# A matmul with rotary embedding: a first read of 64 bytes from every 16th weight row, and weight chunks loaded and multiplied in turn with the first four tiles

## The chip, the cores and the metric

The kernel runs on one core of a Trainium2 chip. The metric is the device time in microseconds of one execution; the median of 13 runs of the kernel before is 154.45 us, from 153.99 to 156.54.

## The reference

```
y = x @ weight                      # x: 16 x 512 x 768, weight: 768 x 768, float32
y -> (batch, seq, 12 heads, 64);  y1, y2 = halves of the 64
out1 = y1 * cos[:, :32] - y2 * sin[:, :32]
out2 = y2 * cos[:, 32:] + y1 * sin[:, 32:]
out  = concat(out1, out2)           # 16 x 512 x 768, float32
```

cos and sin are 512 x 64 and depend on the place in the sequence alone.

## The kernel before, in words

The 8192 rows of x are cut into 64 tiles of 128 rows, handled as 32 pairs. Tile (n, s) is half s of pair n: batch 2 * (n // 4) + s, rows n % 4, n % 4 + 4, and so on. The two tiles of a pair need the same rows of cos and sin.

A tile takes these steps. It is loaded in float32 (`load`, L83, issued on SyncE), cast to float16 (`cast`, L76 on ScalarE, ACT, or L78 on VectorE, DVE), transposed in six blocks on TensorE, PE (`transpose`, L140) and copied from PSUM back to SBUF (L76 or L78). Then six matmuls of 768 columns each, one for each chunk of 128 weight rows, add up in PSUM (`mm`, L177; each is split where a PSUM bank ends, so a tile and a chunk make two instructions). DVE multiplies the result by cos and sin (`products`, L187), GpSimd (POOL) adds the two products (`add`, L204), and a DMA stores the pair (L249). Some later pairs are loaded in another layout and transposed by DVE (L148).

The weight is needed whole: six chunks, named by (t, e), each made of every sixth weight row, (p, t, e) -> row 6p + 2t + e. A chunk is loaded in float32 (`load_w`, L123, SyncE) and cast to float16 on DVE (`cast_w`, L126). So the first tiles can't be finished before the sixth chunk has landed.

Every instruction stands in the order in which the program writes it, on each engine's own queue. DMAs issued on SyncE use eight semaphores in rotation, so from some point on an issue waits until an earlier load has landed. The order of the head is written out by hand:

- SyncE issues x(0,0), x(0,1), x(1,0), x(1,1), then chunk 0 in two parts (columns 0 to 255, then the rest), chunks 1 to 5, cos, sin, and then x(2,0), x(2,1) and so on.
- PE starts with `warm` matmuls on zeros (L259), which compute nothing that is used. They go on between the first transposes, 17 in all.
- Tiles (0,0) and (1,0) are cast and copied by DVE, (0,1) and (1,1) by ACT.
- As each chunk is cast, PE multiplies tiles (0,0) and (0,1) with it, and from the second chunk on also (1,0) with an earlier chunk. What remains of (1,0) and all of (1,1) follows after the sixth chunk. Before the last three chunks of (1,1), `upto("turn", 5)` transposes tile (2,0).

PSUM has six banks for results, three for a pair; pair 2 takes those of pair 0 once DVE has read them. From pair 2 on a loop goes through the pairs; the change does not touch it. POOL reads one column of tile (3,0) (`mark`, L336) before it issues its own first loads (L99) and begins with the additions.

Of the kernel before, what the change touches and what calls it, by code (L numbers as in the profile page):

```python
# [10 lines left out]
FP32 = mybir.dt.float32  # L11
# [6 lines left out]
def kernel(  # L18
# [9 lines left out]
    nc = tc.nc  # L28
    P = nc.NUM_PARTITIONS

    B, S, H = x.shape
# [9 lines left out]
    CHUNKS = [(t, e) for t in range(NT) for e in range(2)]  # L41
# [9 lines left out]
    def where(n, s):  # L51
        return 2 * (n // SB) + s, n % SB

    konst = ctx.enter_context(tc.tile_pool(name="konst", bufs=1))
    ident = konst.tile([P, P], FP16)
    mark = konst.tile([P, 1], FP32)
    cold = konst.tile([P, 512], FP16)
    sin_sb = konst.tile([P, SB, D], FP32)
    csn = konst.tile([P, 2, SB, D], FP32)
# [12 lines left out]
    w_raw, xss, xhs, x16, xTT, psys, tqs, ovs = {}, {}, {}, {}, {}, {}, {}, {}  # L72

    def copy(eng, o, i_):
        if eng is nc.scalar:
            eng.copy(out=o, in_=i_)  # L76
        else:
            eng.tensor_copy(out=o, in_=i_)  # L78

    def load(n, s):  # L80
        b, r = where(n, s)
        xss[n, s] = xpool.tile([P, H], FP32, tag="xs", name="xs")
        nc.sync.dma_start(  # L83
            out=xss[n, s], in_=x[b].rearrange("(p r) h -> r p h", r=SB)[r]
        )

    def load_pair(n):
        for s in (0, 1):
            if n < NP and n not in BLOCKS and n not in BLOCKS_SP:
                load(n, s)  # L90
# [29 lines left out]
    def load_w(t, e, c0=0, c1=H):  # L120
        if c0 == 0:
            w_raw[t, e] = bpool.tile([P, H], FP32, tag="xh", name="w_raw")
        nc.sync.dma_start(out=w_raw[t, e][:, c0:c1], in_=wv[t, e, :, c0:c1])  # L123

    def cast_w(t, e, c0=0, c1=H):
        nc.vector.tensor_copy(out=w_sb[:, t, e, c0:c1], in_=w_raw[t, e][:, c0:c1])  # L126

    def cast(n, s, eng):
        xc = cpool.tile([P, H], FP16, tag="xc", name="xc")
        x16[n, s] = xc  # L130
        src = xss.pop((n, s))
        src = src.rearrange("p (m t e) -> p t m e", t=NT, e=2)
        copy(eng, xc.rearrange("p (t m e) -> p t m e", t=NT, e=2), src)

    def transpose(n, s, eng):
        xc = x16.pop((n, s)).rearrange("p (t m e) -> p t e m", t=NT, e=2)
        bank = pt_pool.tile([P, 8, P], FP16, tag="pt", name="pt")
        pt = bank[:, 0 : 2 * NT].rearrange("p (t e) m -> p t e m", e=2)
        for t, e in CHUNKS:
            nc.tensor.transpose(pt[:, t, e, :], xc[:, t, e, :], ident)  # L140
        xT = tpool.tile([P, NT, 2, P], FP16, tag="xT", name="xT")
        copy(eng, xT, pt)
        xTT[n, s] = xT
# [13 lines left out]
    def psum(n, s):  # L157
        key, banks = (n, 3) if n < NP - ALONE else ((n, s), 2)
        if (n, s) == (NP - 1, 1):
            key, banks = (n, s), 3  # L160
        if key not in psys:
            psys[key] = [
                py_pool.tile([P, 512], FP32, tag="psy", name="psy") for _ in range(banks)
            ]
        ps = psys[key]
        if n >= NP - ALONE:
            cuts = (0, HH, H) if banks == 2 else (0, 5 * D, 10 * D, H)
            return [(b[:, 0 : hi - lo], lo, hi) for b, lo, hi in zip(ps, cuts, cuts[1:])]
        cut = 512 if s == 0 else 256
        return [(ps[s][:, ds(s * 256, cut)], 0, cut), (ps[s + 1][:, 0 : H - cut], cut, H)]  # L170

    def mm(n, s, t, e, c0=0, c1=H):
        for k, (ps, lo, hi) in enumerate(psum(n, s)):
            a, z = max(c0, lo), min(c1, hi)
            if a >= z:
                continue
            nc.tensor.matmul(  # L177
                ps[:, a - lo : z - lo],
                xTT[n, s][:, t, e, :],
                w_sb[:, t, e, a:z],  # L180
                start=((t, e) == CHUNKS[0] and n > 1),
                stop=((t, e) == CHUNKS[-1] and (n > 1 or s >= k)),
            )
# [65 lines left out]
        eng.dma_start(out=dst, in_=src)  # L249


    WARM = 17
    opened = [0]

    def warm(k):
        for _ in range(k):
            n, b = divmod(opened[0] % 6, 3)
            psum(n, 0)
            nc.tensor.matmul(  # L259
                psys[n][b], cold[:, 0:P], cold, start=True, stop=opened[0] < WARM - 6  # L260
            )
            opened[0] += 1

    ctx.enter_context(tc.manual_schedule())

    nc.vector.memset(cold, 0.0)  # L266
    nc.gpsimd.memset(ident, 0.0)  # L267
    nc.gpsimd.affine_select(
        out=ident,
        in_=ident,  # L270
# [3 lines left out]
        pattern=[[-1, P]],  # L274
        channel_multiplier=1,
    )
    for n in (0, 1):
        load_pair(n)
    load_w(0, 0, 0, 256)
    load_w(0, 0, 256, H)  # L280
    for t, e in CHUNKS[1:]:
        load_w(t, e)
    nc.sync.dma_start(out=csn[:, 0], in_=cos.rearrange("(p r) d -> p r d", r=SB))
    nc.sync.dma_start(out=sin_sb, in_=sin.rearrange("(p r) d -> p r d", r=SB))
    for n in range(2, AHEAD - 1):
# [7 lines left out]
    def upto(what, k):  # L293
        while done[what] < min(k, 2 * NP):
            n, s = divmod(done[what], 2)
            done[what] += 1
            if what == "cast":
                if n not in BLOCKS:
                    cast(n, s, nc.scalar)
            elif n in BLOCKS or n in BLOCKS_SP:  # L300
                transpose_blocks(n, s)
            else:
                transpose(n, s, nc.scalar)
# [4 lines left out]
    transpose(0, 0, nc.vector)  # L308
    warm(2)
    transpose(0, 1, nc.scalar)  # L310
    cast(1, 0, nc.vector)
    cast(1, 1, nc.scalar)
    warm(2)
    transpose(1, 0, nc.vector)
    warm(3)
    for c0, c1 in ((0, 256), (256, H)):
        cast_w(0, 0, c0, c1)
        mm(0, 0, 0, 0, c0, c1)
        mm(0, 1, 0, 0, c0, c1)
        if c0 == 0:  # L320
            transpose(1, 1, nc.scalar)
    for k, c in enumerate(CHUNKS[1:]):
        cast_w(*c)
        if k < 2:
            mm(1, 0, *CHUNKS[k])
        mm(0, 0, *c)
        mm(0, 1, *c)
        if 1 < k < 4:
            mm(1, 0, *CHUNKS[k])

    nc.vector.tensor_copy(out=csn[:, 1, :, 0:HD], in_=sin_sb[:, :, HD:D])  # L331
    nc.vector.tensor_scalar_mul(
        out=csn[:, 1, :, HD:D], in0=sin_sb[:, :, 0:HD], scalar1=-1.0
# [4 lines left out]
    load_blocks(BLOCKS[0], (1, 3))  # L338
    rope_pair(0)
    upto("cast", 6)  # L340
    for c in CHUNKS[4:]:
        mm(1, 0, *c)
    for c in CHUNKS[:3]:
        mm(1, 1, *c)
    upto("turn", 5)
    for c in CHUNKS[3:]:
        mm(1, 1, *c)
# [2 lines left out]
    for n in range(2, NP):  # L350
# [7 lines left out]
        for s in (0, 1):  # L358
# [18 lines left out]
            for ps, lo, hi in psum(n, s):  # L377
                for c in CHUNKS:
                    mm(n, s, *c, lo, hi)
                c0, c1 = s * H + lo, s * H + hi  # L380
# [55 lines left out]
```

## Time and profile before

| | |
|---|---|
| median of 13 runs | 154.45 us |
| profiled execution, its time | 154.64 us |
| its span in the profile | 152.9 us |
| PE busy | 145.3 us, 95% |
| DVE busy | 131.1 us, 86% |
| POOL busy | 123.8 us, 81% |
| ACT busy | 73.6 us, 48% |
| DMA | 51.17 MB, mean 335 GB/s |

The span runs from the first instruction to the last; the execution's own time is 1.7 us longer. In the profile a row names the line, the engine, the operation and the tiles it writes and reads; "SPq" is an issue on SyncE's queue, "PEld" the loading of a stationary operand, and the words in square brackets tell how long the engine was idle before and what ended that. The table of windows gives, for each stretch, the busy time of PE, PEld, DVE, ACT and POOL with the number of instructions, then the granted clock of TensorE, the busy share of the DMA engines and the GB/s they moved.

### The profile page before, as it was taken

To read this page: it belongs to the slowest core of one execution; us is meant where nothing else is said; L and a number is where in the kernel's file an instruction comes from. 1 tells how busy PE (TensorE), PEld (TensorE's weight loads), DVE (VectorE), ACT (ScalarE), POOL (GpSimd) and SP (SyncE) were. 2 spreads that over 40 slices of the span, in tenths; PEclk is the share of its full clock that TensorE was granted. 3 is DMA by queue.
4 is the path that set the end of the run, shared out by engine and by line. 5 is a ranking of instruction groups with operands and counts; after the bars stand their busy time and mean duration, and the time that the engine had idled before them with its cause. 6 is when DMAs were issued, how large, how long until landed. Compare 5 with 4: busy or idle time off the path is not lost.

```text
span 152.9 us, 2731 instructions
## 1 busy us (share of the span) xinstructions
PE 145.3 (95%) x1044; PEld 92.4 (60%) x1044; DVE 131.1 (86%) x141; ACT 73.6 (48%) x91; POOL 123.8 (81%) x69
## 2 busy tenths in 40 slices
PE   6989999999999999999999999999999999999950
PEld 2455678665666566666666566666656666666640
DVE  0556999779898998989898989989898989997890
ACT  3340686884344826183535726282616648765200
POOL 1000199999998999799997999787897879999990
PEclk9999999999999999999999999999999999999999
DMA  4999999999999999999999999999999999997554
GB/s 145 350 403 397 404 321 248 296 350 365 331 248 410 322 338 344 337 397 298 370 326 358 379 351 318 358 382 406 264 301 409 414 410 412 412 363 277 219 203 151
DMA packets 29037, 51.17 MB, mean 335 GB/s; under 512 B 7264, under 2 KB 14944, under 8 KB 29024
## 3 DMA queue, kind: packets, MB, share of 16 engines
q1 hardware_dynamic: 16640, 29.04, 56.8%
q10 hardware_dynamic: 6944, 19.99, 33.1%
q0 software_dynamic: 5440, 1.97, 10.7%
q8 instruction: 8, 0.13, 0.3%
q14 instruction: 5, 0.04, 0.1%
HBM read 27.79 MB, written 25.17 MB: 346 GB/s over the span
## 4 chain that ended last, share of the span: by engine, by line
PE 80%; POOL 7%; DMA 5%; SPq 3%; DVE 2%; POOLq 1%; issue 0%; DVEq 0%
PE psy L177 73%; PE pt L140 7%; POOL ov L204 7%; DMA w_raw<-in_weight_dram 5%; SPq L123 1%; DVE tq L187 1%; SPq L83 1%; POOLq L431 1%; DVE w_sb L126 0%; POOLq L204 0%; DVEq L187 0%
## 5 line engine op out<-in xcount | busy, mean ns | idle before, releaser
L177 PE MATMUL psy<-w_sb,xT 128*128 128x256 f16 (+3 forms) x787 | 131.5, 322 | 0.6 <-DVE w_sb L126 0.6
L187 DVE TENSOR_TENSOR tq<-psy,csn 128x1024 f32<-128x1024 f32 (+2 forms) x100 | 112.2, 1164 | 9.4 <-PE psy L177 9.1
L204 POOL TENSOR_TENSOR ov<-tq 128x1536 f32<-128x1536 f32 (+3 forms) x42 | 111.6, 2679 | 7.8 <-DVE tq L187 5.2
L177 PEld LDWEIGHTS <-xT 128*128 128x128 f16 x787 | 75.2, 98 | 45.3 <-issue 0.8
L76 ACT COPY xT<-pt 128x768 f16<-128x768 f16 x38 | 30.4, 799 | 58.6 <-PE pt L140 58.6
L76 ACT CAST xc<-xs 128x768 f16<-128x768 f32 x38 | 33.0, 903 | 9.5 <-DMA xs<-in_x_dram 8.8
L140 PE MATMUL pt<-ident,xc 128*128 128x128 f16 x240 | 20.2, 221 | 0.5 <-DVE xc L78 0.5
L140 PEld LDWEIGHTS <-xc 128*128 128x128 f16 x240 | 16.9, 99 | 6.2 <-DVE xc L78 1.5
L336 POOL COPY mark<-xs 128x1 f32<-128x1 f32 x1 | 0.2, 185 | 16.6 <-DMA xs<-in_x_dram 16.6
L76 ACT CAST xc<-xf 128x768 f16<-128x768 f32 x14 | 12.7, 907 | 0.0
L99 POOL DMA_DIRECT2D xh<-in_x_dram x20 | 11.8, 595 | 0.5 <-issue 0.5
L148 DVE STREAM_TRANSPOSE xT<-xc 128x384 f32<-128x384 f32 x14 | 7.9, 562 | 0.0
L259 PE MATMUL psy<-cold 128*128 128x512 f16 x17 | 6.5, 528 | 1.2 <-DVE cold L266 1.2
L148 DVE STREAM_TRANSPOSE xT<-xh 128x384 f32<-128x384 f32 x10 | 7.0, 704 | 0.0
L126 DVE CAST w_sb<-w_raw 128x768 f16<-128x768 f32 (+2 forms) x7 | 3.5, 502 | 2.3 <-DMA w_raw<-in_weight_dram 2.2
L78 DVE CAST xc<-xs 128x768 f16<-128x768 f32 x2 | 1.9, 952 | 3.2 <-DMA xs<-in_x_dram 3.1
L259 PEld LDWEIGHTS <-cold 128*128 128x128 f16 x17 | 1.9, 127 | 3.5 <-issue 2.2
L78 DVE COPY xT<-pt 128x768 f16<-128x768 f16 x2 | 1.1, 558 | 1.6 <-PE pt L140 1.6
L76 ACT ACT_TABLE_LOAD x1 | 1.3, 1283 | 0.7 <-PEq L417 0.7
L266 DVE MEMSET cold<- 128x256 uint32 x1 | 0.3, 272 | 0.9 <-PEq L417 0.9
L267 POOL MEMSET ident<- 128x128 f16 x1 | 0.2, 205 | 0.3 <-POOLq L417 0.3
L331 DVE COPY csn<-sin_sb 128x128 f32<-128x128 f32 x1 | 0.2, 227 | 0.2 <-DMA sin_sb<-in_sin_dram 0.2
(9 smaller groups left out, 1.8 us busy)
## 6 DMA issues: line engine op xcount, KB each, us to landing
out_dram<-ov ACTq DMA_DIRECT2D x25, 768.0 KB, 8.8
xs<-in_x_dram SPq DMA_DIRECT2D x40, 384.0 KB, 8.6
xf<-in_x_dram SPq DMA_DIRECT2D x28, 192.0 KB, 8.6
out_dram<-ov SPq DMA_DIRECT2D x7, 384.0 KB, 2.3
out_dram<-ov SPq DMA_DIRECT2D x3, 768.0 KB, 6.4
w_raw<-in_weight_dram SPq DMA_DIRECT2D x5, 384.0 KB, 7.2
xh<-in_x_dram POOLq DMA_DIRECT2D x20, 96.0 KB, 10.6
out_dram<-ov ACTq DMA_DIRECT2D x1, 320.0 KB, 2.2
```

The lines of the kernel that those rows point to most:

```text
L76: eng.copy(out=o, in_=i_)
L78: eng.tensor_copy(out=o, in_=i_)
L83: nc.sync.dma_start(out=xss[n, s], in_=x[b].rearrange("(p r) h -> r p h", r=SB)[r])
L99: eng.dma_start(out=dst[ts(q, R)], in_=src[r, q])
L123: nc.sync.dma_start(out=w_raw[t, e][:, c0:c1], in_=wv[t, e, :, c0:c1])
L126: nc.vector.tensor_copy(out=w_sb[:, t, e, c0:c1], in_=w_raw[t, e][:, c0:c1])
L140: nc.tensor.transpose(pt[:, t, e, :], xc[:, t, e, :], ident)
L148: nc.vector.transpose(out=xT.bitcast(FP32).rearrange("p t (j a) o -> p t j (a o)", j=NQ), in_=x16.pop((n, s)).bitcast(FP32).rearrange(orde ...
L177: nc.tensor.matmul(ps[:, a - lo : z - lo], xTT[n, s][:, t, e, :], w_sb[:, t, e, a:z], start=((t, e) == CHUNKS[0] and n > 1), stop=((t, e) ...
L187: nc.vector.tensor_tensor(out=tq.rearrange("p j (h d) -> p j h d", d=D), in0=ps.rearrange("p (h d) -> p h d", d=D) .unsqueeze(1).broadcast ...
L204: eng.tensor_tensor(out=ovs[n][:, ds(c0, w)].rearrange("p (h t d) -> p h t d", t=2, d=HD), in0=tq[:, 0].rearrange("p (h t d) -> p h t d", ...
L259: nc.tensor.matmul(psys[n][b], cold[:, 0:P], cold, start=True, stop=opened[0] < WARM - 6)
```

## The change

ACT issues a small DMA before anything else: 16 floats from every 16th row of the weight, 48 rows, into a tile `touch` that nothing reads. The loads are issued in another order: x(0,0), x(0,1), chunk 0 (in one load), x(1,0), chunk 1, x(1,1), chunks 2 to 5; what follows is as before. The number of bytes loaded is the same but for the 3 KB of the touch.

The program of the head follows that order. Tile (1,0) is cast by ACT instead of DVE. PE makes 14 warming matmuls instead of 17, all ahead of the first chunk; two further matmuls on zeros (`idle`) add nothing to a bank that is in use, ahead of the transposes of (1,0). Chunk 0 is multiplied with (0,0) and (0,1) before (1,0) is transposed, chunk 1 before (1,1) is; (1,0) takes chunks 0 to 2 and (1,1) chunks 0 and 1 while later chunks arrive. After the sixth chunk (1,1) takes chunk 2, (1,0) takes chunks 3 to 5, tile (2,0) is transposed, and (1,1) takes chunks 3 to 5.

```diff
+    touch = konst.tile([3 * 16, 16], FP32)
...
-    WARM = 17
+    WARM = 14
...
+    def idle(k):
+        for _ in range(k):
+            nc.tensor.matmul(psys[1][2], cold[:, 0:P], cold, start=False, stop=False)
...
+    nc.scalar.dma_start(
+        out=touch, in_=weight.rearrange("(a b) n -> b a n", b=16)[0, :, 0:16]
+    )
...
-    for n in (0, 1):
-        load_pair(n)
-    load_w(0, 0, 0, 256)
-    load_w(0, 0, 256, H)
-    for t, e in CHUNKS[1:]:
-        load_w(t, e)
+    load_pair(0)
+    for k, c in enumerate(CHUNKS):
+        load_w(*c)
+        if k < 2:
+            load(1, k)
...
     transpose(0, 1, nc.scalar)
-    cast(1, 0, nc.vector)
+    warm(WARM - 12)
+    cast_w(*CHUNKS[0])
+    mm(0, 0, *CHUNKS[0])
+    mm(0, 1, *CHUNKS[0])
+    cast(1, 0, nc.scalar)
+    cast_w(*CHUNKS[1])
+    idle(2)
+    transpose(1, 0, nc.vector)
+    mm(0, 0, *CHUNKS[1])
+    mm(0, 1, *CHUNKS[1])
     cast(1, 1, nc.scalar)
-    warm(2)
-    transpose(1, 0, nc.vector)
-    warm(3)
-    for c0, c1 in ((0, 256), (256, H)):
-        cast_w(0, 0, c0, c1)
-        mm(0, 0, 0, 0, c0, c1)
-        mm(0, 1, 0, 0, c0, c1)
-        if c0 == 0:
-            transpose(1, 1, nc.scalar)
-    for k, c in enumerate(CHUNKS[1:]):
-        cast_w(*c)
-        if k < 2:
-            mm(1, 0, *CHUNKS[k])
+    cast_w(*CHUNKS[2])
+    for c in CHUNKS[:2]:
+        mm(1, 0, *c)
+    transpose(1, 1, nc.scalar)
+    for k, c in enumerate(CHUNKS[2:]):
+        if k:
+            cast_w(*c)
         mm(0, 0, *c)
         mm(0, 1, *c)
-        if 1 < k < 4:
-            mm(1, 0, *CHUNKS[k])
+        if k == 0:
+            mm(1, 0, *c)
+        elif k < 3:
+            mm(1, 1, *CHUNKS[k - 1])
...
     upto("cast", 6)
-    for c in CHUNKS[4:]:
+    mm(1, 1, *CHUNKS[2])
+    for c in CHUNKS[3:]:
         mm(1, 0, *c)
-    for c in CHUNKS[:3]:
-        mm(1, 1, *c)
     upto("turn", 5)
```

## The prediction

> **What bounds the kernel now.** I read the page's chain that ended last first, then the same chain in order of time, then the first 20 us piece by piece. The chain gives PE 80% of the span, and in order of time it is one run of matrix work between two short ends:
>
> ```profile
> PE 80%; POOL 7%; DMA 5%; SPq 3%; DVE 2%; POOLq 1%; issue 0%; DVEq 0%
> ...
> 5.04 7.19 DMA w_raw<-in_weight_dram
> 12.23 0.02 issue
> 12.25 0.57 DVE w_sb L126
> 12.82 0.04 issue
> 12.86 4.40 PE psy L177 x26
> 17.26 0.34 PE pt L140 x6
> ...
> 134.78 0.99 PE psy L177 x6
> ```
>
> From 12.86 us on, TensorE never waits until its work is nearly over (matmuls end at 147.5 us); a few microseconds of last products, additions and a store follow. The windows from 20 to 124 us have PE busy for all 104 us. Nothing in the change touches that stretch, so the whole question is how many microseconds earlier or later TensorE enters it. What it waits for there is the load stream, and the SyncE queue tells when each load lands, because from the eighth on each issue waits for the load eight before it:
>
> ```profile
> 6.88 0.33 SPq L123 DMA_DIRECT2D w_raw<-in_weight_dram  x1
> 8.32 0.33 SPq L283 DMA_DIRECT2D csn<-in_cos_dram  x1
> 8.70 0.43 SPq L284 DMA_DIRECT2D sin_sb<-in_sin_dram  x1
> 9.32 0.33 SPq L83 DMA_DIRECT2D xs<-in_x_dram  x1
> 10.29 0.33 SPq L83 DMA_DIRECT2D xs<-in_x_dram  x1
> ...
> 14.21 0.33 SPq L83 DMA_DIRECT2D xs<-in_x_dram  x1
> ```
>
> These are the landings of x(1,0), x(1,1), the two parts of weight chunk 0, chunk 1 and chunk 5; x(0,0) and x(0,1) are read off the first casts, 4.28 and 5.21. So the steps between 384 KB loads are 0.93, **1.67, 1.44**, 1.00 (chunk 0 in two parts), 0.97 and then four more that end at 14.21, (14.21 - 9.32) / 5 = 0.98 each. Against 0.98, the third and fourth loads lose 0.69 + 0.46 = **1.15 us**. The load rate dips in just those microseconds:
>
> ```profile
> 4.00:6.00 2.00, 2.00 (x10) 0.97 (x9) 0.95 (x1) 0.79 (x1) 0.00 (x0) 1.00 1.02 349
> 6.00:8.00 2.00, 1.53 (x15) 0.81 (x14) 1.51 (x2) 0.90 (x2) 0.00 (x0) 1.00 0.96 341
> 8.00:10.00 2.00, 1.80 (x19) 1.25 (x18) 1.19 (x3) 0.88 (x2) 0.00 (x0) 1.00 1.03 402
> 10.00:12.00 2.00, 1.82 (x12) 0.98 (x11) 1.12 (x2) 0.80 (x1) 0.00 (x0) 1.00 1.03 415
> ```
>
> The last column is GB/s. At 405, the 4 us would have moved 1620 KB; they moved 1380, which is 240 KB or 0.6 us for an average engine of the 16. A load has landed when its slowest engine is done, so the slowest lost 1.15 and the average 0.6. The dip ends when weight data flow.
>
> The last rows say why the landings decide and the order of the matmuls nearly does not:
>
> ```profile
> 15.92 0.90 ACT L76 CAST xc<-xs 128x768 f16<-128x768 f32 x1 [5.13 <-DMA xs<-in_x_dram]
> ...
> 17.72 0.79 ACT L76 COPY xT<-pt 128x768 f16<-128x768 f16 x1
> ...
> 18.56 0.55 PEld L177 LDWEIGHTS <-xT 128*128 128x128 f16 x6 [0.37 <-ACT xT L76]
> ```
>
> ScalarE gets x(2,0) from the load stream at 15.92, x(2,1) at 16.91, and only then copies the transposed x(2,0), to 18.51; TensorE's weight load for tile (2,0) starts at 18.56, having waited on that copy. TensorE had other work up to then, so there is no gap, but no slack either.
>
> **The change part by part.** Sums are made on the profiled execution, 154.64 us (span 152.9, so 1.7 around it), and moved by -0.19 to the median, 154.45.
>
> *Reordered multiplication.* The same 24 pairs of tile and chunk are computed for tiles (0,0) to (1,1); a pair costs 2 x 5.85 / 36 = 0.325 us (36 matmuls in 5.85 in the chain). With all landings as before, chunk 0 lands third, at 6.9, and x(1,0) fourth, at 8.3. The last chunk is cast at 14.21 + 0.56 = 14.77; by then 15 pairs can be done (before: 14); two more to 15.4, then four, and the transposes of (2,0) could start at 16.7, against 17.26 now. But their cast ends at 15.92 + 0.90 = 16.82, and the copy that ends at 18.51 hangs on x(2,1), not on TensorE. So the new order alone buys at most 18.56 - 18.51 = 0.05. It does buy more if the loads come earlier, since then nothing of TensorE's is in their way: the landing shift of x(2,1) comes through whole.
>
> *Work moved between engines.* x(1,0) is cast on ACT (0.9) where DVE did it (0.95). ACT's chain is then cast (0,1), copy, casts (1,0) and (1,1) (at 8.3 and 10.3), copy of (1,1) by about 12.6; next is x(2,0) at 15.9, so 3 us hide it. On DVE the copy of the transposed (1,0) now stands behind the cast of chunk 1: with chunk 1 landing at 9.3 that cast ends at 9.9, and the transposes it copies end at 9.75; 0.15 us, and TensorE's own next step waits for chunk 1 anyway. Were chunk 1 a microsecond late, this copy and x(1,0)'s matmuls would be late with it.
>
> *Filler.* Three warming matmuls go and two `idle` ones come, 0.81 / 3 = 0.27 each. The two lie between chunk 0's work (to about 8.2) and the transposes of (1,0), which wait for ACT until 9.2: hidden. TensorE's share from 7 to 12 us falls from about 0.85 to 0.7; I cost that at nothing as long as the clock stays up. If it did not, matmuls would run at the rate of the first ten in the timeline (4.45 / 10 = 0.45 us for 512 columns against 0.27): about 1 us over the twelve pairs before chunk 4.
>
> *Chunk 0 in one load.* 1.00 against 0.98: 0.02 earlier.
>
> *The touch.* On ACT one issue of 0.4 us (SyncE's take 0.42) stands before the table load, which ends at 2.02 and would end at 2.5; ACT's first cast is at 5.21: hidden. On SyncE the wait of chunk 3's issue is now for the touch instead of for x(0,0); it could issue at about 4.1 and has eight loads in flight behind it, so a touch that takes 3 us is still hidden. On the 16 DMA engines its 48 packets, three each if shared evenly, go beside the first packets of x(0,0). The nearest row for a small packet is the software queue: 10.7% of 16 x 152.9 us over 5440 packets, 48 ns. Three are 0.14 us, and everything after it lands 0.14 later. From the other side: the half-microsecond windows from 2.0 to 3.5 move 197, 252 and 332 GB/s where the next moves 406, a starting loss of 218 KB or 0.54 us; touching the weights might cost that again in front, 0.54, or a straggler's 1.15. I take 0.14, as the packets run beside x(0,0)'s own starting loss.
>
> What it may take away is the 1.15. That belongs to the weights if an engine reading ahead meets the new tensor while it still finishes x(1,0) and x(1,1); for it speaks that the dip ends as weight data flow, against it that no weight load itself is slow (1.00, 0.97). Upper bound 1.15. If engines only become alike, the straggler falls back to the average: 1.15 - 0.6 = 0.55. Net 0.55 to 1.15, less 0.14, plus 0.02: 0.43 to 1.03. I take **0.65**, nearer the lower end, since part of the dip may be x's own. Everything downstream follows: cos and sin stand in the same stream, DVE's first products come with them, and DVE waits 9.1 us on PE later, so it can keep up; ACT waits 56.8 us on PE's transposes after 17 us.
>
> One rule speaks against it. By the Trainium skill, "DMA: Bandwidth & Descriptors", section "The descriptor swizzle", a 128-partition load gives each engine two groups of four partitions, 32 apart. By "Why a DMA increments its semaphore by 16 and not by 1" there, a 48-partition transfer gives three partitions to each engine. An engine would then touch 48 neighbouring weight rows, and mostly load others; if what is cold is kept per engine, the touch warms the wrong ones and the time is that of the first rival. The trace before names no engine and cannot settle it.
>
> **The rivals.** *The dip is not the weights'* (x(1,0) and x(1,1) pay it in their new places, or the first microseconds of any stream do). Then x(2,1) lands 0.14 - 0.02 = 0.12 later, the reordering gives back 0.05: 154.45 + 0.07, about **154.5**, within 0.3 to either side. For it: the chunk loads themselves show no loss.
>
> *The touch is paid in front.* Its cold reads hold the engines before x(0,0) and nothing is won later, or chunk 0, now third in the stream, brings a fresh tensor into the straggler's path all the same. Price 0.54 to 1.15, I take 0.6: **155.05**. It decides once x(2,1) lands later than 16.9 + 0.46; TensorE has no slack there (0.05). For it: the 0.54 that x(0,0) pays for starting. Against: 3 KB beside 384 KB.
>
> **How the numbers follow.** Forecast 154.64 - 0.65 = 153.99, less 0.19: **153.8**, chance 0.44. No real change 0.26, the touch in front 0.30. A measurement of this kernel can tell about 0.3%, 0.46 us. Faster by more than that 0.44, within it 0.26, slower 0.30. The forecast's upper end, 1.03, with 0.3 for unlike runs gives 153.1 below; the middle of the slow rival's price, 0.85, gives 155.3 above. Outside lie the clock's fall and a straggler paid twice.
>
> **What would show it.** The landings of the 384 KB loads after the second: steps near 1.0 throughout and x(2,1)'s cast by 16.3 bear the forecast out; two steps of 1.4 to 1.7 still there, wherever they stand, are the first rival; x(0,0)'s cast later than 4.6 is the second. The chain should enter unbroken PE work with chunk 3 or 4 and the weight load of tile (2,0) should start near 17.9 instead of 18.56. It is wrong if the landings improve and that load does not, or if PE waits after 20 us.

## The result and the profile after

The changed kernel took **157.86 us** (median of its runs, 155.61 the lowest), against 154.46 for the kernel before on the same chip. The ratio is **1.0145, 95% interval 1.011 to 1.018**; like every ratio below it leaves out runs that were disturbed (two of e1_tile's ten took 222 and 543 us), so it is smaller than the quotient of the medians. The kernel is slower; forecast were 153.8 us and a range of 153.1 to 155.3. The profiled execution took 155.61 us with a span of 153.6, 0.7 above the span before: it is one of the better runs and shows the loss at its smallest.

The same views as before. First the chain that ended last, shares by engine and by line, from the page:

```profile
PE 54%; DMA 30%; POOL 7%; ACT 2%; SPq 2%; DVE 1%; issue 1%; POOLq 1%; ACTq 0%; DVEq 0%
PE psy L178 49%; DMA xs<-in_x_dram 16%; DMA xf<-in_x_dram 9%; POOL ov L205 7%; PE pt L141 5%; DMA out_dram<-ov 5%; ACT xT L77 2%; DVE tq L188 1%; SPq L84 1%; ACT xc L77 1%; SPq L124 1%; POOLq L445 1%; ACTq L250 0%; SPq L100 0%; ACTq L77 0%
```

PE had 80% of this chain before and DMA 5%. In order of time (start, us, what) the 33 us from 49.7 on are three transfers, one behind the other, and then ScalarE:

```profile
49.21 0.35 PE pt L141 x6
49.69 7.12 DMA out_dram<-ov
57.24 13.37 DMA xf<-in_x_dram
70.62 11.64 DMA xs<-in_x_dram
82.34 0.38 ACTq L250
82.81 0.81 ACT xT L77
83.66 6.02 PE psy L178 x36
...
91.77 0.79 ACT xT L77
92.61 6.02 PE psy L178 x36
```

A store; a load that SyncE could issue only when that store had landed, since it stands in SyncE's queue behind one that waits for the store; a load, x(19,1), that it could issue only when the former had landed; and a store of ACT's, store(12), that waited for the latter. That store is the key to the stop of PE. On ACT's timeline (start, busy, what; in brackets how long ACT was idle and what ended it), after:

```profile
77.67 1.71 ACT L77 CAST xc<-xs 128x768 f16<-128x768 f32 x2 [1.82 <-POOL ov L205]
82.34 0.38 ACTq L250 DMA_DIRECT2D out_dram<-ov  x1
82.81 0.80 ACT L77 COPY xT<-pt 128x768 f16<-128x768 f16 x1 [3.43 <-DMA xs<-in_x_dram]
```

and the same place in the kernel before:

```profile
75.95 1.70 ACT L76 CAST xc<-xs 128x768 f16<-128x768 f32 x2
80.08 0.38 ACTq L249 DMA_DIRECT2D out_dram<-ov  x1
81.44 0.80 ACT L76 COPY xT<-pt 128x768 f16<-128x768 f16 x1 [3.79 <-PE pt L140]
```

The copy that feeds PE's next tile stands behind the store in ACT's queue. The waits themselves are not new: by the semaphores in the traces, store(12) waits for x(19,1) in the kernel before as well, and that load for the same earlier load and store. Before, x(19,1) landed at 80.01, the store went out at 80.08, and the copy waited for PE alone. Now it lands at 82.26, 2.25 us later, the store goes at 82.34, and the copy and PE wait. The quarter load ahead of x(19,1) took 13.37 us from issue to landing, against 10.41 before. Nine microseconds on it happens again, with store(14) and a load that landed at 91.20 instead of 89.50. PE's weight loads, after, show what it costs, 0.41 + 0.47 = 0.88 us in this run:

```profile
83.66 5.64 PEld L178 LDWEIGHTS <-xT 128*128 128x128 f16 x36 [0.41 <-ACT xT L77]
...
92.61 0.44 PEld L178 LDWEIGHTS <-xT 128*128 128x128 f16 x4 [0.47 <-ACT xT L77]
```

The head, which the prediction was about, is hardly changed. SyncE's issues give the landings of chunk 0, x(1,0) and chunk 1 (6.37, 7.76, 8.99); tile (2,0)'s weight load still waits on the copy:

```profile
5.40 0.33 SPq L124 DMA_DIRECT2D w_raw<-in_weight_dram  x1
6.37 0.33 SPq L293 DMA_DIRECT2D csn<-in_cos_dram  x1
7.76 0.33 SPq L294 DMA_DIRECT2D sin_sb<-in_sin_dram  x1
8.99 6.33 SPq L84 DMA_DIRECT2D xs<-in_x_dram  x8
```

```profile
18.35 0.55 PEld L178 LDWEIGHTS <-xT 128*128 128x128 f16 x6 [0.60 <-ACT xT L77]
```

18.35 against 18.56: the head is **0.21 us earlier**, and the kernel lost everything after 80 us.

### The profile page after: what moved, and what is told of

The parts are those of the page before. It is cut to its first block, busy times and chain, and to the rows that moved or that the text cites. A ratio compares the mean times of both kernels' runs of the same rounds, so it can differ in the third digit from the quotient of the medians.

```text
span 153.6 us, 2723 instructions
## 1 busy us (share of the span) xinstructions
PE 145.2 (95%) x1042; PEld 91.5 (60%) x1042; DVE 130.2 (85%) x139; ACT 74.6 (49%) x92; POOL 123.8 (81%) x69
## 4 chain that ended last, share of the span: by engine, by line
PE 54%; DMA 30%; POOL 7%; ACT 2%; SPq 2%; DVE 1%; issue 1%; POOLq 1%; ACTq 0%; DVEq 0%
PE psy L178 49%; DMA xs<-in_x_dram 16%; DMA xf<-in_x_dram 9%; POOL ov L205 7%; PE pt L141 5%; DMA out_dram<-ov 5%; ACT xT L77 2%; DVE tq L188 1%; SPq L84 1%; ACT xc L77 1%; SPq L124 1%; POOLq L445 1%; ACTq L250 0%; SPq L100 0%; ACTq L77 0%
## 5 line engine op out<-in xcount | busy, mean ns | idle before, releaser
L77 ACT CAST xc<-xs 128x768 f16<-128x768 f32 x39 | 34.0, 903 | 14.0 <-DMA xs<-in_x_dram 8.1
L141 PEld LDWEIGHTS <-xc 128*128 128x128 f16 x240 | 16.4, 98 | 6.6 <-ACT xc L77 1.6
L127 DVE CAST w_sb<-w_raw 128x768 f16<-128x768 f32 x6 | 3.3, 558 | 4.3 <-DMA w_raw<-in_weight_dram 4.3
L260 PE MATMUL psy<-cold 128*128 128x512 f16 x14 | 5.1, 516 | 1.2 <-DVE cold L276 1.2
L79 DVE CAST xc<-xs 128x768 f16<-128x768 f32 x1 | 1.0, 952 | 3.3 <-DMA xs<-in_x_dram 3.3
L268 PE MATMUL psy<-cold 128*128 128x512 f16 x2 | 0.6, 379 | 0.0
```

The source lines that it names most:

```text
L260: nc.tensor.matmul(psys[n][b], cold[:, 0:P], cold, start=True, stop=opened[0] < WARM - 6)
```

## The theories

The kernel before and the changed one differ in three things behind the first microseconds: where tiles lie in SBUF (64 bytes for `touch`), the order of the loads, and the order in which casts, transposes and matmuls of the first four tiles are written. The last one also decides in which order the framework plans all later DMAs, and that order has an effect of its own. The eight semaphores of the front section are shared by SyncE's loads and ACT's stores: a DMA may only be issued when the DMA eight places ahead of it in the plan has landed. From the compiled programs, the eight DMAs planned behind store(0), the first store:

```
before    x(7,0)  x(7,1)  xf     store(1)  xf  x(9,0)    x(9,1)  store(2)
after     x(7,0)  x(7,1)  xf     store(1)  xf  x(9,0)    store(2) x(9,1)
g4_store  x(7,0)  x(7,1)  extra  xf        xf  store(1)  x(9,0)  x(9,1)
```

("xf" is a quarter of a pair loaded in the other layout.) The eighth waits for store(0). Before, it is a store of ACT's own; after, it is SyncE's load of x(9,1), with all later loads behind it in SyncE's queue. The profiles show it. SyncE's issues, before:

```profile
25.71 0.33 SPq L99 DMA_DIRECT2D xf<-in_x_dram  x1
27.02 1.44 SPq L83 DMA_DIRECT2D xs<-in_x_dram  x2
29.36 2.04 SPq L99 DMA_DIRECT2D xf<-in_x_dram  x2
```

and after:

```profile
28.96 0.33 SPq L100 DMA_DIRECT2D xf<-in_x_dram  x1
30.64 5.66 SPq L84 DMA_DIRECT2D xs<-in_x_dram  x2
36.35 1.57 SPq L100 DMA_DIRECT2D xf<-in_x_dram  x2
```

The two issues of x(9,0) and x(9,1) are 1.1 us apart before (27.02 and 28.12) and 5.3 after (30.64 and 35.95); in the trace store(0) lands at 35.89. Call this the **rotation** theory. Its rivals: the addresses; the touch; the new load order, which goes with one DMA engine falling behind; and the compute order itself. (The trace counts a load's landing in 16 marks, read here as one for each DMA engine: x(5,1) has landed on its last engine at 23.90 us before and at 25.53 after, on the median engine at 22.07 and 22.51.)

## The experiments

One number per kernel tells where its time went: how much later than in the kernel before the same matmul starts, matmuls counted from the last, at places that lie at 20, 80 and 100 us in the kernel before. The first column is the head, the rest stops of PE. Each row is one profiled run, so the head's column has a scatter of its own (rows that have the head of before differ by 0.45). e1_tile and e4_tail, whose profiled runs took 543.41 and 158.97 us, have no row.

| kernel | 20 us | 80 us | 100 us | ratio to before, 95% |
|---|---|---|---|---|
| after | -0.21 | -0.21 | 0.68 | 1.0145 [1.011, 1.018] |
| e2_touch | -0.29 | -0.29 | -0.29 | 1.001 [0.997, 1.005] |
| e3_order | 0.27 | 0.27 | 2.03 | 1.017 [1.0135, 1.0205] |
| f3_loads | 0.97 | 0.97 | 0.97 | 1.010 [1.003, 1.017] |
| f4_compute | 0.20 | 0.21 | 0.36 | 1.0115 [1.007, 1.016] |
| f2_act | -0.35 | -0.35 | 1.26 | 1.0035 [1.000, 1.007] |
| g4_store | -0.18 | 0.43 | 5.42 | 1.0336 [1.030, 1.037] |
| g3_before | -0.42 | -0.42 | -0.42 | 0.9963 [0.994, 0.999] |
| g2_compute | 0.26 | 0.26 | 0.82 | 1.012 [1.006, 1.018] |
| g1_after | -0.09 | -0.09 | -0.02 | 1.0054 [1.002, 1.009] |
| h2_compute2 | 0.54 | 0.54 | 1.96 | 1.0073 [1.003, 1.011] |
| h1_after2 | -0.48 | -0.48 | -0.48 | 1.0064 [1.002, 1.0105] |
| k1_after | -0.34 | -0.34 | -0.34 | 0.9978 [0.995, 1.001] |
| k2_before | 0.03 | 0.03 | 0.03 | 0.9963 [0.993, 0.999] |

Every loss behind the head falls between 70 and 100 us.

**The addresses** (e1_tile): the kernel before with the 48 x 16 tile of the change, which moves everything behind it by 64 bytes, and no read of the weight.

```diff
+    touch = konst.tile([3 * 16, 16], FP32)
...
+    nc.gpsimd.memset(touch, 0.0)
```

> The kernel before with the 64-byte tile alone: allocated where the change puts it and zeroed once by POOL, so that every later tile lies 64 bytes further on; no touch, no new order. Theory A (the lasting loss comes from the moved addresses: loads that fall behind in the middle, so that PE waits for transposed tiles): about 156.5, PE waiting on ACT's copies after 20 us. Theory B (the loss comes from the new order of loads and casts, and the waits that go with it): 154.5. Theory C (the touch itself): 154.5.

Measured 155.56 us, ratio 1.0015 [0.997, 1.006]. The addresses are not it. And the same tile put behind all others in the changed kernel (e4_tail), so that every address is that of before:

```diff
-    touch = konst.tile([3 * 16, 16], FP32)
...
+    tail = ctx.enter_context(tc.tile_pool(name="tail", bufs=1))
+    touch = tail.tile([3 * 16, 16], FP32, tag="touch", name="touch")
```

> The changed kernel with the tile of the touch placed behind all others, so that no address moves. A: about 154.2. B and C: 156 to 158, as the changed kernel.

156.86 us, 1.0139 [1.011, 1.017]: the loss stays with the old addresses.

**The touch alone** (e2_touch): the kernel before, with the touch into a tile behind all others and chunk 0 in one load.

```diff
+    nc.scalar.dma_start(
+        out=touch, in_=weight.rearrange("(a b) n -> b a n", b=16)[0, :, 0:16]
+    )
...
-    load_w(0, 0, 0, 256)
-    load_w(0, 0, 256, H)
+    load_w(0, 0)
```

> The kernel before with the touch, its tile placed behind all others so that no address moves, and chunk 0 in one load so that the number of DMAs stays; order of loads and multiplication as before. A: 154.5. B: 154.5. C: 156.5 or more. For the head: if the dip of 1.15 us belongs to the weights' first reads, the steps between landings fall to about 1.0 and x(2,1) lands near 15.9 instead of 16.9, 153.6.

154.77 us, 1.001 [0.997, 1.005]: nothing. The dip that it was to take away is still there: in the trace x(0,1), x(1,0), x(1,1) and chunk 0 have landed at 5.04, 6.60, 7.96 and 9.02, steps of 1.56, 1.36 and 1.06.

**The orders without the touch** (e3_order): the changed kernel without the touch and its tile, chunk 0 in two loads.

```diff
-    nc.scalar.dma_start(
-        out=touch, in_=weight.rearrange("(a b) n -> b a n", b=16)[0, :, 0:16]
-    )
...
-        load_w(*c)
+        if k == 0:
+            load_w(0, 0, 0, 256)
+            load_w(0, 0, 256, H)
+        else:
+            load_w(*c)
```

> The changed kernel without the touch and its tile, chunk 0 in two loads so that the number of DMAs stays; addresses as in the kernel before. A: about 154.3 (the 0.2 us won in the head stay). B: 156 to 158, PE waiting in the middle. C: 154.3. For the head: if the touch earns anything, chunk 0 and x(1,0) land later than the 6.4 and 7.8 of the changed kernel.

157.08 us, 1.017 [1.0135, 1.0205]. The whole loss is in the orders; x(9,1) is issued at 36.58 us here.

**The load order alone** (f3_loads), the program of the head as before:

```diff
-    for n in (0, 1):
-        load_pair(n)
+    load_pair(0)
     load_w(0, 0, 0, 256)
     load_w(0, 0, 256, H)
-    for t, e in CHUNKS[1:]:
+    load(1, 0)
+    load_w(*CHUNKS[1])
+    load(1, 1)
+    for t, e in CHUNKS[2:]:
```

> The kernel before with the load order alone changed: x(0,0), x(0,1), chunk 0 in two parts, x(1,0), chunk 1, x(1,1), chunks 2 to 5; casts, transposes and matmuls in their old order, and every later load and store on the DMA semaphore it had before. Theory D (the new load order leaves one DMA engine further behind, and the load stream never makes that up): about 157, x(5,0) landing near 23.9 instead of 22.1. Theory E (the new order of casts makes the program give later loads other DMA semaphores, so that SyncE's load of x(9,1) waits for the first store): 154.5 to 155, x(9,1) issued near 28.

155.83 us, 1.010 [1.003, 1.017]. I first took this for the lagging DMA engine, since x(5,1) is complete only at 25.63 us. The table says otherwise: all of it is lost in the head, 0.97, and PE never stops again. It is a misfit of order. PE's waits in the head (who waits for whom: us, times, longest) show it:

```profile
PEld L140 <- DVE xc L78: 2.6, 1, 2.6
PE pt L140 <- DVE xc L78: 2.1, 1, 2.1
```

The old program transposes (1,0) before it multiplies anything, and x(1,0) now comes two loads later. In the changed kernel the program moved with the loads, so this loss isn't in it.

**The compute order alone** (f4_compute): the new casts, transposes and matmuls on the old load order, no touch. In the plan x(9,1) waits for store(0), as after.

```diff
-    load_pair(0)
-    for k, c in enumerate(CHUNKS):
-        load_w(*c)
-        if k < 2:
-            load(1, k)
+    for n in (0, 1):
+        load_pair(n)
+    load_w(0, 0, 0, 256)
+    load_w(0, 0, 256, H)
+    for t, e in CHUNKS[1:]:
+        load_w(t, e)
```

> The new order of casts, transposes and matmuls with the old load order, no touch. Its later loads and stores have the DMA semaphores of the changed kernel. D: 154.5 to 155, x(5,0) landing near 22.1. E: about 157, the load of x(9,1) issued near 36 because it waits for the first store.

156.52 us, 1.0115 [1.007, 1.016]; its runs lie in two groups, 155.2 to 156.0 and 157.1 to 157.2. x(9,1) is issued at 36.35.

**One cast moved** (f2_act): the kernel before, x(1,0) cast by ACT. It leaves the head nearly alone and gives the semaphores a third arrangement, in which x(9,1) waits for no store.

```diff
-    cast(1, 0, nc.vector)
+    cast(1, 0, nc.scalar)
```

> The kernel before with one word changed: x(1,0) is cast by ACT instead of DVE. Load order as before; this alone gives the DMA semaphores a third arrangement, in which x(7,0)'s load comes ahead of the first store and x(9,1)'s ahead of the third. D: 154.5. E: not 157, since no load of pair 9 waits for a store; some tenths either way from other waits, ACT having 0.9 us more to do in the head with 3 us to spare.

154.97 us, 1.0035 [1.000, 1.007]. The profiled run, its slowest (156.17), has x(5,1) complete at 25.35 with the old load order, and PE stops for 1.61 us in all between 85 and 95 us. So the lagging engine isn't tied to the new load order, and PE can stop without x(9,1) waiting for store(0).

**The wait added to the kernel before** (g4_store): one 3 KB load, issued by ACT behind store(0), shifts the rotation by one, and x(9,1) falls on store(0)'s semaphore. The program is otherwise that of before, but every later DMA moves in the rotation too: 13 of SyncE's loads wait for a store, against 11 before.

```diff
+        if n == 4:
+            nc.scalar.dma_start(out=extra, in_=cos[0 : 3 * 16, 0:16])
         load_pair(n + AHEAD - 2)
```

> The kernel before, with one more load of 3 KB (48 rows of 64 bytes of cos into a tile that nobody reads), issued by ACT after store(0). By the rotation of the eight semaphores, SyncE's load of x(9,1) then falls on the semaphore of store(0) and has to wait for that store's landing; the load order and the compute order of the first tiles are those of before. Theory of the rotation: x(9,1) is issued at about 36.6 us instead of 28.1, the blocks behind it 7 to 8 us later, PE waits after 40 us, and the ratio to before is 1.007 to 1.015. Rival (the wait is harmless, and the kernel with the new compute order alone is slow because of its compute order): 154.5 us, ratio 1.00, within 0.3%, although x(9,1) is late.

159.92 us, **1.0336** [1.030, 1.037], two to five times the loss that I expected. x(9,1) goes out at 36.60. The chain of this kernel in order of time, from the store on:

```profile
28.18 8.35 DMA out_dram<-ov
36.60 6.55 DMA xs<-in_x_dram
43.25 11.05 DMA out_dram<-ov
54.32 12.55 DMA xs<-in_x_dram
66.89 4.89 DMA xf<-in_x_dram
71.84 0.91 ACT xc L78
72.79 0.51 PE pt L142 x6
```

Loads and stores alternate, each held by the one before, and at 71.84 PE's stops begin. The added wait is on this chain; since the rotation behind it has moved as well, the run doesn't price that wait alone. Its control, the same load issued by SyncE ahead of x(9,0) (g3_before), which makes x(9,1) wait for x(7,0):

```diff
+        if n == 4:
+            nc.sync.dma_start(out=extra, in_=cos[0 : 3 * 16, 0:16])
         load_pair(n + AHEAD - 2)
```

> The control to the other three: the kernel before, with the same 3 KB load issued by SyncE ahead of the loads of x(9,0) and x(9,1). The rotation then gives x(9,1) the semaphore of the load x(7,0), which has long landed; no SyncE load waits for a store ahead of 36 us. Both theories: 154.5 us, ratio 0.998 to 1.003. If this alone is slower by over 0.5%, the 3 KB load has a price of its own and the other three have to be read against this kernel.

154.04 us, 0.9963 [0.994, 0.999], runs from 153.72 to 154.40. So the small load has no price that shows, and this place for it even helps: in the kernel before, another load waits for store(1) until 39.33 us; here ACT's store(3) has that place.

**The wait taken out of the new orders**, first with one small load of SyncE's, the same diff as in the control (g2_compute from f4_compute, g1_after from the changed kernel):

> The kernel with only the new cast, transpose and multiplication order of the first four tiles (156.52 us, ratio 1.0115), with the 3 KB load issued by SyncE ahead of x(9,0) and x(9,1), which moves x(9,1) from the semaphore of store(0) to that of the load x(7,0). Theory of the rotation: x(9,1) issued at about 30 instead of 36.35 us, 154.3 to 155.0 us, ratio 0.999 to 1.004. Rival (the compute order itself costs the time): still about 156.5, ratio 1.01.

> The changed kernel with the same 3 KB load ahead of x(9,0) and x(9,1), so that x(9,1) no longer waits for store(0). Two causes (rotation, and the load order that leaves one DMA engine behind): the load order's share stays, x(5,0) still lands near 23.8 us, x(9,1) is issued at about 31 instead of 35.95 us, 155.6 to 156.3 us, ratio 1.007 to 1.012. If the rotation were the only cause, 154.4, ratio 1.000. If it has no part, 156.7, ratio 1.0145.

g2_compute 156.32 us, 1.012: no gain, against the rotation theory as I had put it. But the wait had not gone, it had moved: a quarter load (xf) behind x(9,1) had become the eighth DMA behind store(1), and went out at 40.30 us, after that store's landing at 40.28. g1_after 155.48, 1.0054 [1.002, 1.009], about a third of the loss left, although the same wait had moved there too (40.54, after 40.53): the moved wait alone doesn't explain why one gained and the other did not. With a second small load behind x(9,1) and x(9,0) no SyncE load waits for a store ahead of 42 us:

```diff
         if n == 4:
             nc.sync.dma_start(out=extra, in_=cos[0 : 3 * 16, 0:16])
         load_pair(n + AHEAD - 2)
+        if n == 4:
+            nc.sync.dma_start(out=extra2, in_=cos[0 : 3 * 16, 0:16])
```

> The new cast, transpose and multiplication order of the first four tiles on the old load order, now with two 3 KB loads on SyncE, one ahead of x(9,0) and x(9,1) and one behind them. With one of them the wait for store(0) had only gone over to a wait for store(1), by the next quarter of a block, at 33 to 40 us; with two, store(2) follows store(0) on its semaphore and store(3) store(1), both on ACT, and no SyncE load waits for a store ahead of 42 us. Theory of the rotation: 153.9 to 154.8 us, ratio 0.996 to 1.002, no long SyncE wait for a store between 30 and 41 us. Rival (the compute order itself costs it): 156.3 again, ratio 1.01.

> The changed kernel with the same two 3 KB loads, so that no SyncE load waits for a store ahead of 42 us. What then remains over the other kernel of this call is the new load order (and the 64-byte reads, which were worth nothing). Theory of two causes: x(5,1) is still complete only at about 25.6 us, and the ratio stays at 1.004 to 1.009. Rival (the load order only costs through the late issues that the store waits add to): 154.0 to 154.8, ratio 0.997 to 1.002.

h2_compute2 155.45 us, 1.0073 [1.003, 1.011]; h1_after2 155.89, 1.0064 [1.002, 1.0105]. A part came back, not all. h2_compute2 met neither of its expectations; h1_after2's ratio lies in the range of the one that left the new load order as a second cause, and k1_after, below, tests that again. Both have two groups of runs: h1_after2 154.4 to 154.8 and 155.8 to 156.8, h2_compute2 154.9 to 155.5 and 156.9 to 157.0. The profiled run of h1_after2 is of its lower group and has no stop of PE, that of h2_compute2 of its upper group and has two, which end at 92.75 and 99.73 us. What h2_compute2's lower group lost was not profiled.

**All the waits taken out** (k1_after): in the plan of the changed kernel 14 SyncE loads wait for a store and 17 stores of ACT's wait for a load. Ten small loads, placed so that as few SyncE loads as possible stand behind a store, bring this to 3 and 6.

```diff
+    BEFORE, BEHIND = {3: 1, 5: 1, 9: 1, 14: 1, 17: 1}, {4: 1, 9: 1, 12: 1, 14: 1, 18: 1}
+
+    def pad(k):
+        for _ in range(k):
+            extra = tail.tile([3 * 16, 16], FP32, tag="extra", name="extra")
+            nc.sync.dma_start(out=extra, in_=cos[0 : 3 * 16, 0:16])
...
+        pad(BEFORE.get(n, 0))
         load_pair(n + AHEAD - 2)
+        pad(BEHIND.get(n, 0))
```

> The changed kernel with ten 3 KB loads on SyncE between tiles 3 and 18, placed so that each store's semaphore goes next to another store or to one of these loads' neighbours whose predecessor is a load: no SyncE load waits for a store until the last three tiles. Theory of the rotation as the whole loss behind the head: no stop of PE between 20 and 140 us, 153.9 to 154.9 us, ratio 0.996 to 1.002, and the runs of 156 us and more, seven of twelve in the kernel with two such loads, are gone. Rival (something else in the new order, such as the DMA engine that falls behind, stops PE): some runs stay at 156 to 157 us and the ratio at 1.005 or more. [...]

**154.47 us, 0.9978 [0.995, 1.001]**, twelve runs from 154.02 to 155.44: the loss is gone, and so is the upper group. The orders, the touch and the addresses are those of the changed kernel, so none of them costs this time without the waits. On ACT's timeline store(12), which now waits for another store, goes out early and the copy waits for PE again:

```profile
78.10 0.38 ACTq L258 DMA_DIRECT2D out_dram<-ov  x1
81.10 0.80 ACT L78 COPY xT<-pt 128x768 f16<-128x768 f16 x1 [3.79 <-PE pt L149]
```

SyncE's own waits from 19 to 120 us (for whom: us in total, times, longest) name a store twice, 2.2 us, where the changed kernel has 25.5 us in eleven waits:

```profile
SPq L85 <- DMA out_dram<-ov: 1.6, 1, 1.6
...
SPq L108 <- DMA out_dram<-ov: 0.6, 1, 0.6
```

```profile
SPq L84 <- DMA out_dram<-ov: 16.6, 7, 5.5
...
SPq L100 <- DMA out_dram<-ov: 8.9, 4, 3.3
```

The kernel before has 33.4 us in eleven such waits (20.2 and 13.2) and is faster than the changed one all the same: their sum alone doesn't decide. Nor does the lateness of the loads: x(19,1) lands at 83.20 in k1_after, later than the 82.26 of the changed kernel, and PE doesn't stop. A late load costs time where a store, with a copy behind it, waits for it. The profiled runs whose semaphores are those of before or of after, where store(12) waits for x(19,1), bear that out. The store went out at 80.08 before, at 80.37 in e2_touch and at 81.81 in f3_loads (PE 0.97 us late from the head), with no stop of PE; at 81.89 in f4_compute, with 0.15 us of stops between 80 and 100 us; at 82.34 after, with 0.88; at 83.23 in e3_order, with 1.76.

The same treatment of the kernel before (k2_before, eleven small loads at other places, 3 waits left instead of 11):

> The kernel before with eleven such loads, which leave one SyncE load waiting for a store between the head and the last tiles instead of eight. Theory of the rotation: 153.6 to 154.3 us, ratio 0.993 to 0.998, as in the kernel with one such load (0.9963), and with less spread than before. Rival (SyncE's waits for stores matter only at 31 to 41 us): no better than 0.9963; or the eleven loads cost more than they free: above 1.000.

154.33 us, 0.9963 [0.993, 0.999], no better than with one small load. Without these waits the two orders are alike, 154.47 and 154.33; the fastest versions of this study are the kernel before with one or with eleven small loads.

## Why the prediction was wrong

**The step that failed** is the sentence on the windows from 20 to 124 us, "Nothing in the change touches that stretch", with the conclusion that the whole question is when TensorE enters it. PE was busy for all 104 us there, but its supply had little slack (the issue of store(12) ended at 80.46 before, 0.98 us ahead of the copy behind it), and the change does touch the supply: it rearranges the plan of the DMAs, and through eight shared semaphores that puts more of SyncE's loads behind ACT's stores (14 instead of 11), while ACT's stores, with the copies queued behind them, stand behind loads. What the runs showed in the place of that step: PE stopped for 0.88 us behind 80 us in the profiled run and for 1.76 in e3_order, and with nearly all these waits taken out, and all orders kept, the loss was gone (0.9978). The prediction stated the rotation itself, and used it to read landings, but followed it only for loads and only through the head ("the wait of chunk 3's issue is now for the touch"). The list of planned DMAs, to be had before any run, showed that x(9,1) had come to wait for store(0). Its price could have been bounded: store(0) lands at 36.56 us before, x(9,1) was issued at 28.12, so up to 8 us for the load stream; g4_store, with this wait and the shifted rotation behind it, lost 5.6 us behind the head.

**The touch and the dip.** The dip did not go, as the first rival said. In the changed kernel the landings of x(0,1), chunk 0, x(1,0), chunk 1 and x(1,1) are 0.97, 1.39, 1.23 and 1.07 apart: against 0.98 that is 0.41 + 0.25 + 0.09 = 0.75 lost instead of 1.15, and x(0,1) itself came 0.19 later (5.40 against 5.21). The 0.65 became 0.21, and even that is within the scatter of the head. e2_touch shows that it is not the touch's doing. The touch's own cost, 0.14, can't be told from nothing. The rule that was weighed against it (the Trainium skill, "DMA: Bandwidth & Descriptors", section "The descriptor swizzle") made it the time of the first rival, and the head went that way. No run here shows that the touch reached the wrong engines, nor that anything in the weights is cold.

**The rest of the working held.** The landing shift of x(2,1) comes through whole: cast at 16.70 instead of 16.91 and the weight load 18.35 instead of 18.56, 0.21 both. The reordering as such buys next to nothing (with the old load order, in f4_compute, the head is 0.20 later, within its scatter). The cast of (1,0) on ACT, the copy on DVE and the missing filler cost nothing that shows; the granted clock is 1.00 in the windows from 4 to 12 us and from 20 to 124. The last line of the prediction named the sign to look for, "if PE waits after 20 us", without a mechanism behind it and so without a chance of its own.

**The slow rival** had its number near the truth of the best runs, 155.05, but for a reason that isn't there: x(0,0)'s cast came at 4.41, below its 4.6, and x(2,1) landed earlier, not later. That nearness is luck.

**What stays open.** k1_after takes away waits in both directions, loads behind stores and stores behind loads; how the loss divides between them, and which single wait of the new plan matters most, was not separated. In particular it is not shown that the wait of x(9,1) for store(0) is what made the loads late in the changed kernel's profiled run. x(7,0), which waits for no store, already landed at 32.51 there against 29.34 before: 15 of its 16 marks were in by 29.50, the last came 3 us later. k1_after has the same (32.17), and its x(13,0) lands at 54.09 us, no earlier than the 53.96 of the changed kernel, without that wait. So the lagging engine may have made the loads late, and the waits made that cost time.

Why the same kernel has runs with and without a stop (h1_after2) was not settled. The kernel before has such a spread too: 6 of its 48 runs are above 156 us. Of the 34 runs of g3_before, k1_after and k2_before none is above 155.5.

## What to carry to other kernels

When DMAs of several queues share completion semaphores in rotation, list for every load which earlier DMA it has to wait for, in the new program against the old, before costing anything else: an edit of the head can move a load behind a store 15 us later, and others after it, and the loss can show as a stop of the matrix engine at 80 us. A busy engine tells nothing about the slack of its supply; look for who waits for whom one queue further back, and what stands behind the waiting instruction in its own queue. And a test that removes a wait has to be looked at for where the wait went: here the first attempt moved it to the next store.

## What was not expected of the hardware

A store of 768 KB beside a full load stream takes long to land: store(0) from its issue at 28.36 us to 36.56 before. That is what makes waiting for one so dear.

One DMA engine, if the marks are read so, can be 3 to 4 us behind the median one for a load (x(5,1): 22.37 on the median engine and 25.58 on the last in k1_after, 21.99 and 26.03 in k2_before) without any cost to these kernels, which have few of the waits: neither stops after the head, though in the kernel before the last engine was done at 23.90. What delays that engine was not found.

Two kernels with the same loads, stores and matmuls, one of the loads, of 3 KB, in another queue and place, differ by 3.8% (159.92 against 154.04 us, g4_store and g3_before).
